# A decoder layer: the cached keys of four sequences turned by VectorE in 32x32 squares and scored on sixteen array tiles

## The chip, the cores and the metric

The kernel runs on one core of one Trainium2 chip. The metric is the device time of one execution in microseconds (us). The engines are named as the profile names them: PE (TensorE, matrix multiplications), PEld (its weight loads), DVE (VectorE), ACT (ScalarE), POOL (GpSimd) and SP (SyncE, which issues nearly all the transfers).

## The reference

The kernel is one step of one decoder layer, for a prompt of 512 rows and for eight sampled sequences of four rows each. The layer is a hybrid mixer (four mLSTM heads beside four heads of differential attention), cross-attention into 256 memory tokens, and a gated MLP with a causal convolution. The change is in the differential attention of the sampled sequences. Each of them has 256 cached rows of keys in two pages, found through a page table, and four new ones:

```python
past_k = cache_dk[l][page_table].reshape(Bs, past_len, DA_HEADS, 2, DA_QK_DIM)   # 8, 256, 4, 2, 64
...
def diff_attend(q, k, v, mask, lam):
    s = jnp.einsum('bqhcd,bkhcd->bhcqk', q.astype(jnp.float32), k.astype(jnp.float32)) * (DA_QK_DIM ** -0.5)
    s = jnp.where(mask[None, None, None], s, -jnp.inf)
    p = jax.nn.softmax(s, axis=-1)
    a = p[:, :, 0] - lam * p[:, :, 1]
    return jnp.einsum('bhqk,bkhd->bqhd', a, v.astype(jnp.float32))
```

A head has 128 numbers in a key: two components of 64. A query gives a score with each component. With four heads, two components and four rows there are 32 rows of scores for each sequence, and 260 columns.

## The kernel before

The kernel is written as Python generators that a framework records in program order; it then sorts the instructions of each engine by priority, adds the semaphores, and each engine runs its own list in that order. Nothing overtakes within an engine, so an instruction that waits holds those behind it.

The stage around the change lies at 247 to 304 us. Two pipelines run in it, one step of each in turn. `pipe(n, *stages)` runs stage s of item t - s in step t, the last stage first.

- The prompt pipeline has 16 items, one for each block of 128 query rows and each head. `da_soft` (L1202) scores both components into two PSUM tiles `sda` (L1211, with the causal mask added by L1212); DVE takes the negated maximum of each (`nm`, L1214), ACT the exponential (`pda`, L1215), and DVE combines both components: the reciprocal (L1217), the coefficient `rc` (L1218) and `pda` (L1219). Two steps later `da_turn` transposes `pda` on PE (`tpa`, L1227), and one more step later `da_av` multiplies by the values (`oda`, L1237). After each fourth item `da_post` normalises (`dasq`, `dass`, `dat`, `dtm`). The key range grows with the block: 128, 256, 384 and 512 columns.
- The pipeline of the cached keys has eight items, one for each sequence. `dk_load` gathers its two pages into a staging tile. `dk_turn` (L1185) transposes them on PE, eight transposes of 128x128 into the PSUM tiles `tpk` (L1191), which ACT and DVE copy to `kT` (L1192). POOL adds the four new keys (L1187). `dk_scores` (L1194) multiplies with `qz`, the queries laid out with zeros so that both components come out of one multiplication: four multiplications, one for each head, on four column tiles of the array (`ssc`, L1197). DVE adds the mask of the four new columns (L1199) and takes the maximum (`snm`, L1035); ACT takes the exponential into `das` (L1036).

When all eight sequences are done, `sample_softmax` makes the coefficients on DVE (`scf`, L1042 to L1045; `csz`, L1046), and PE combines the scores of all sequences (`spa`, L1055). ACT copies the result (`spc`, L1057), DVE makes `pz` from it (L1261), PE transposes both (`spt`, `npn`), ACT lays them out (`daz`), and the loop over the values begins (`ops`, L1279), with the prompt's remaining steps in between. Then comes the output projection, whose weights (`w_out`) are loaded into the same staging tiles.

The slots `kT` come from the pool `wp`, four slots of 8 KB per partition that hold the weights in the other stages (`wslot`). In this stage the weights may use two of them.

## Time and profile before

| | |
|---|---|
| Median of three runs | 957.77 us (955.96 to 959.61) |
| The profiled execution | 956.79 us, its span 955.0 us |
| Busy in the span | PE 932.7, PEld 810.6, DVE 599.2, ACT 388.8, POOL 197.5 us |
| The clock granted to PE | 0.993 over the span, 1.00 in this stage |
| Transfers | 130.27 MB, 136 GB/s on average |

The span is the stretch between the first and the last instruction that the profiler recorded. Busy time is the sum of the stretches in which an engine had an instruction under way. Matrix multiplications are pipelined, so that a busy PE need not be PE at its peak; the distance from the start of one group to the start of the next says what a group holds PE for. Idle time of an engine counts only where another engine waits for it.

### The profile page before, as it was taken

The page shows a single profiled execution, that of the slowest core. Times are in us where ns is not written, and L with a number is a line of the kernel's source. Part 1 is how long each engine was busy: PE and PEld are TensorE (multiplying, and loading weights), DVE is VectorE, ACT ScalarE, POOL GpSimd, SP SyncE. Part 2 cuts the span into 40 slices and gives each one's busy share as a digit, 9 for nine tenths or more (in the row PEclk, how much of TensorE's full clock was granted, in tenths as well). Part 3 has the DMA queues.
Part 4 walks back from the last instruction along what each step waited for, and adds up shares of the span by engine and source line. Part 5 has one row for each costly group of instructions (what it writes and reads, how often), then busy time and mean ns, then how long its engine had stood idle before and what let it go on. Part 6 is the DMA issues. An engine that isn't in the chain of part 4 may idle for free. (4 is left out here: it accounts for less than half of the span.)

```text
span 955.0 us, 17088 instructions
## 1 busy us (share of the span) xinstructions
PE 932.7 (98%) x6619; PEld 810.6 (85%) x6619; DVE 599.2 (63%) x1129; ACT 388.8 (41%) x750; POOL 197.5 (21%) x383
## 2 busy tenths in 40 slices
PE   8999999999999999999999999999999999999995
PEld 5899777879866778998777799989988997999974
DVE  5745144565887448635654769727758676676867
ACT  5655133344676447624544523332212222222232
POOL 6610000024432217300000444001110110111114
PEclk9999999999999999999999999999999999999998
DMA  8950023334825429955953743063053302512023
GB/s 278 309 184 2 1 89 136 89 110 150 264 90 183 155 94 329 307 155 167 353 213 114 206 134 89 4 177 89 4 144 79 122 26 79 165 48 89 24 92 116
DMA packets 120674, 130.27 MB, mean 136 GB/s; under 512 B 8568, under 2 KB 86233, under 8 KB 120593
## 3 DMA queue, kind: packets, MB, share of 16 engines
q1 hardware_dynamic: 114408, 125.69, 41.9%
q10 hardware_dynamic: 6184, 3.48, 1.2%
q8 instruction: 52, 0.85, 0.4%
q14 instruction: 30, 0.24, 0.1%
HBM read 112.22 MB, written 16.93 MB: 135 GB/s over the span
## 5 line engine op out<-in xcount | busy, mean ns | idle before, releaser
L146 ACT CAST wslot<-wst 128x1024 fp32r<-128x1024 f32 x125 | 130.9, 1050 | 259.9 <-issue 74.7
L477 PE MATMUL mm<-fT,wslot 128*128 128x256 f32 x1872 | 235.9, 288 | 0.0
L477 PEld LDWEIGHTS mm<-fT,wslot 128*128 128x128 f32 x1872 | 234.4, 188 | 1.8 <-issue 0.8
L147 DVE TENSOR_TENSOR wslot<-wst,wslot 128x1024 fp32r<-128x1024 f32 x125 | 155.1, 1245 | 89.3 <-ACT wslot L146 88.8
L1691 PE MATMUL mm<-wslot,act 128*128 128x512 f32 (+1 forms) x180 | 70.2, 391 | 0.0
L1692 PE MATMUL mm<-wslot,act 128*128 128x512 f32 (+1 forms) x180 | 70.0, 392 | 0.0
L1690 PE MATMUL mm<-wslot,act 128*128 128x512 f32 (+1 forms) x180 | 69.3, 387 | 0.0
L1598 POOL COPY cvo<-u 128x2 f32<-128x2 f32 x43 | 11.0, 256 | 204.8 <-DVE u L1596 194.7
L407 PE MATMUL mm<-wslot,hT 128*128 128x512 f32 x128 | 52.2, 408 | 0.0
L409 PE MATMUL mm<-wslot,hT 128*128 128x512 f32 x128 | 51.5, 403 | 0.0
L408 PE MATMUL mm<-wslot,hT 128*128 128x512 f32 x128 | 51.3, 401 | 0.0
L477 PE MATMUL mm<-hT,wslot 128*128 128x256 f32 (+1 forms) x384 | 51.0, 289 | 0.0
L1593 DVE TENSOR_TENSOR u<-mm,rsb 128x256 f32<-128x256 f32 x43 | 18.2, 424 | 51.0 <-PE mm L477 50.1
L477 PEld LDWEIGHTS mm<-hT,wslot 128*128 128x128 f32 x384 | 49.2, 188 | 0.5 <-issue 0.2
L1690 PEld LDWEIGHTS mm<-wslot,act 128*128 128x128 f32 x180 | 34.3, 191 | 8.0 <-issue 0.8
L1691 PEld LDWEIGHTS mm<-wslot,act 128*128 128x128 f32 x180 | 33.8, 188 | 7.2
L1692 PEld LDWEIGHTS mm<-wslot,act 128*128 128x128 f32 x180 | 33.8, 188 | 7.2 <-issue 0.4
L1610 ACT ACTIVATE c<-c 128x560 f32<-128x560 f32 x21 | 14.1, 672 | 56.7 <-DVE c L1604 56.7
L1604 DVE SCALAR_TENSOR_TENSOR c<-u,cvT,c 128x560 f32<-128x560 f32 x43 | 34.3, 798 | 0.9
L1603 DVE SCALAR_TENSOR_TENSOR c<-u,cvT,c 128x560 f32<-128x560 f32 x43 | 34.1, 793 | 0.2
L1703 DVE TENSOR_TENSOR yp<-mm,yp 128x512 f32<-128x512 f32 (+1 forms) x41 | 27.2, 674 | 5.1 <-PE mm L1692 5.0
L409 PEld LDWEIGHTS mm<-wslot,hT 128*128 128x128 f32 x128 | 24.5, 191 | 5.3
(474 smaller groups left out, 1857.7 us busy)
## 6 DMA issues: line engine op xcount, KB each, us to landing
wst<-in_w_up_dram SPq DMA_DIRECT2D x42, 512.0 KB
wst<-in_w_in_dram SPq DMA_DIRECT2D x28, 512.0 KB
wst<-in_w_down_dram SPq DMA_DIRECT2D x20, 512.0 KB
wst<-in_cache_mem_k_dram SPq DMA_DIRECT2D x16, 512.0 KB
wst<-in_w_mk_dram SPq DMA_DIRECT2D x8, 512.0 KB
xb<-in_x_prompt_dram SPq DMA_DIRECT2D x8, 512.0 KB
wst<-in_cache_dk_dram SPq DMA_DIRECT2D x16, 256.0 KB
wst<-in_cache_dv_dram SPq DMA_DIRECT2D x16, 256.0 KB
```

Source lines behind the costliest of these rows:

```text
L146: nc.scalar.copy(out=hi, in_=src)
L147: (eng or nc.vector).tensor_tensor(out=lo, in0=src, in1=f32(hi), op=SUB)
L407: mm(ps[b], lhsT=xt.hi(k, c0, c0 + n), rhs=s[:, 0, kk, :], start=(k == 0), stop=False)
L408: mm(ps[b], lhsT=xt.hi(k, c0, c0 + n), rhs=s[:, 1, kk, :], start=False, stop=False)
L409: return mm(ps[b], lhsT=xt.lo(k, c0, c0 + n), rhs=s[:, 0, kk, :], start=False, stop=(k == nk - 1))
L477: mm(ps[i], lhsT=s[:, l, k, :], rhs=x(k, c0, c1), start=(k == 0 and j == 0), stop=(k == 7 and j == 2))
L1603: STT(out=c, in0=u[:, 1:EXT - 1], scalar=w[1], in1=c, op0=MUL, op1=ADD)
L1604: STT(out=c, in0=u[:, 0:EXT - 2], scalar=w[0], in1=c, op0=MUL, op1=ADD)
L1690: mm(ps, lhsT=t[:, 0, c0:c0 + P], rhs=s[:, 0, i % 2, cs], start=st, stop=False)
L1691: mm(ps, lhsT=t[:, 0, c0:c0 + P], rhs=s[:, 1, i % 2, cs], start=False, stop=False)
L1692: return mm(ps, lhsT=t[:, 1, c0:c0 + P], rhs=s[:, 0, i % 2, cs], start=False, stop=en)
L1703: VTT(out=y, in0=ps, in1=y, op=ADD)
```

## The change

For sequences 4 to 7, and for these alone, the keys are no longer turned on PE. `dk_turn` issues one instruction of DVE, which turns the staging tile of 128x1024 in squares of 32x32 into `kq`, one sequence in each prompt step, placed behind the last `nm` of that step. A square's rows are then 32 of the 128 numbers of a head, and the four quarters of the partitions hold different cached rows. So `dk_quads`, in the step in which sequence 7 was scored before, multiplies for all four sequences at once: 64 multiplications of 32x32 weights with 256 columns, on sixteen tiles of the array, four quarters of the numbers added up in PSUM. For each of the four row tiles there is a PSUM tile `ssq` of its own. Four small multiplications score the 16 new keys.

The scores are copied out of PSUM to `das` by ACT and DVE, two tiles each; DVE adds the mask, takes one maximum for the four sequences, and ACT takes four exponentials out of SBUF.

The queries must lie on all four quarters of the partitions for that: `qrep`, a tile of the pool `npool`, is filled through DRAM, one write and four reads, issued by SP. And `kq` takes the place of two of the four weight slots: the pool `wp` is closed at the start of the stage and opened again as `wa` and `wb` of two slots each, `wb` gives way to `kq` for sequences 4 to 7 and comes back behind `dk_quads`. The `kT` of sequences 0 to 3 use the two slots of `wb`.

In `da_soft` the coefficient `rc` is made by a `scalar_tensor_tensor` with one pointer scalar instead of a `tensor_scalar` with two.

```diff
     def dk_turn(b):
-        kt = kts[b] = wp.tile([P, H, 260], F32, name="kT", tag="W")
+        if b >= 4:
+            if b == 4:
+                closed("wb")
+                opened("k", 1)
+                kq.append(lay["k"][1].tile([P, 4, 2, 512], F32, name="kq", tag="K"))
+            with tc.issue_after(dve_last[0]):
+                nc.vector.transpose(kq[0][:, b - 4].rearrange("p g n -> p (g n)"), kst[b][2])
+            return
+        kt = kts[b] = slot([P, H, 260], F32, "kT", "wb")
...
+    qrep = N("qrep", 512).rearrange("p (h j n) -> p h j n", h=H, j=4)
+    qz_d = dram.tile([P, H, NS], F32, name="qz_d")
+    dma(out=qz_d, in_=qz[:, :, 1].rearrange("p h c r -> p h (c r)"))
+    for i in range(4):
+        dma(out=qrep[NS * i:NS * i + NS], in_=qz_d.rearrange("(j q) h n -> q h j n", q=NS))
+
+    def dk_quads():
+        ps = [(at if i else mmp)("ssq") for i in range(4)]
+        kt = kq[0].rearrange("p b g (j r) -> p (b g) j r", r=NS)
+        t = pe_last[0]
+        for j in range(4):
+            for i in range(4):
+                r = slice(NS * i, NS * i + NS)
+                for h in range(H):
+                    with burst(t):
+                        t = mm(ps[i][NS * h:NS * h + NS, :256], lhsT=qrep[r, h, j, :], rhs=kt[r, :, 4 * h + j, :],
+                               start=(j == 0), stop=(j == 3)).ins
+        pn = ps[0][:, 256:272]
+        for h in range(H):
+            with burst(t):
+                t = mm(pn[NS * h:NS * h + NS], lhsT=qz[:, h, 1].rearrange("p c r -> p (c r)"), rhs=dkT[:, h, SEQ + 16:SEQ + 32],
+                       start=True, stop=True).ins
+        VTT(out=sall[:, 4:8, 256:260], in0=v2(pn, TS), in1=con("cm4").unsqueeze(1).broadcast_to([P, 4, TS]), op=ADD)
+        for i in range(4):
+            (VCP if i % 2 else nc.scalar.copy)(out=sall[:, 4:8, :256].rearrange("p b (c i r) -> p b c i r", c=2, i=4)[:, :, :, i, :],
+                                               in_=ps[i][:, :256].rearrange("p (b c r) -> p b c r", c=2, r=NS))
+        VRED(out=nm[:, 4:8], in_=sall[:, 4:8, :], axis=AX.X, op=MAX, negate=True)
+        for b in range(4, 8):
+            ACT(out=sall[:, b, :], in_=sall[:, b, :], func=AF.Exp, bias=nm[:, b:b + 1], accum_out=su[:, b:b + 1])
+        closed("k")
+        opened("wb", NSLOT - 2)
+        slots_in("wb", "wb", "wa", "wa")
+
     def dk_scores(b):
+        if b >= 4:
+            if b == 7:
+                dk_quads()
+            return
...
-        VTS(out=rc[:, 1:2], in0=rc[:, 1:2], scalar1=su[:, 0:1], scalar2=nlam, op0=MUL, op1=MUL)
+        STT(out=rc[:, 1:2], in0=rc[:, 1:2], scalar=nlam, in1=su[:, 0:1], op0=MUL, op1=MUL)
...
     W.nslots = 2
+    closed("w")
+    opened("wa", 2)
+    opened("wb", NSLOT - 2)
+    slots_in("wa")
```

Three places of the engines' lists show what moves (the new kernel's lines are 70 to 75 higher than the old one's).

PE, from the prompt scores of the step in which sequence 7 is scored. First before, then now:

```order
L1211 MATMUL sda<-dkT,dqz 128x384
L1212 LDWEIGHTS cb
L1212 MATMUL sda<-cb 128x128
L1197 MATMUL ssc<-kT,qz 32x260 x4
L1237 MATMUL oda<-dvN,aT 128x128 x2
L1227 MATMUL tpa<-cpk,pda 128x128 x2
L1211 MATMUL sda<-dkT,dqT 128x384
```

```order
L1281 MATMUL sda<-dkT,dqz 128x384
L1282 LDWEIGHTS cb
L1282 MATMUL sda<-cb 128x128
L1240 MATMUL ssq<-kq,qrep 32x256 x64
L1245 MATMUL ssq<-dkT,qz 32x16 x4
L1307 MATMUL oda<-dvN,aT 128x128 x2
L1297 MATMUL tpa<-cpk,pda 128x128 x2
L1281 MATMUL sda<-dkT,dqT 128x384
```

The last sequence's four multiplications have given way to the 68 of the four sequences; the prompt's work around them is as it was, and between it and `spa` stand the same two prompt steps.

DVE, two prompt steps in the middle of the stage. First before (a copy of `kT`, the mask and the maximum of a sequence among the prompt's work), then now:

```order
L1192 COPY kT<-tpk 128x4x128
L1214 TENSOR_REDUCE nm<-sda 128x1
L1199 TENSOR_TENSOR ssc<-ssc,cpk 128x4
L1035 TENSOR_REDUCE snm<-ssc 128x1
L1214 TENSOR_REDUCE nm<-sda 128x1
L1217 RECIPROCAL rc<-su 128x2
L1214 TENSOR_REDUCE nm<-sda 128x1
L1218 TENSOR_SCALAR rc<-rc,su,nlam 128x1
```

```order
L1284 TENSOR_REDUCE nm<-sda 128x1 x2
L1212 STREAM_TRANSPOSE kq<-wst 128x1024
L1287 RECIPROCAL rc<-su 128x2
L1284 TENSOR_REDUCE nm<-sda 128x1
L1288 SCALAR_TENSOR_TENSOR rc<-rc,nlam,su 128x1
L1284 TENSOR_REDUCE nm<-sda 128x1
L1212 STREAM_TRANSPOSE kq<-wst 128x1024
L1289 SCALAR_TENSOR_TENSOR pda<-pda,rc 128x256
```

In each step one long turn stands where a copy, a mask and a maximum stood.

DVE, from the step in which sequence 7 is scored to `csz`. First before, then now:

```order
L1035 TENSOR_REDUCE snm<-ssc 128x1
L1217 RECIPROCAL rc<-su 128x2
L1218 TENSOR_SCALAR rc<-rc,su,nlam 128x1
L1219 SCALAR_TENSOR_TENSOR pda<-pda,rc 128x384
L1042 RECIPROCAL scf<-ssu 128x8
L1214 TENSOR_REDUCE nm<-sda 128x1
L1044 TENSOR_SCALAR scf<-scf,cv 128x8
L1214 TENSOR_REDUCE nm<-sda 128x1
L1045 TENSOR_TENSOR scf<-scf,cpk 128x8
L1046 TENSOR_TENSOR csz<-cpk,scf 128x4x2x16
```

```order
L1289 SCALAR_TENSOR_TENSOR pda<-pda,rc 128x384
L1249 COPY das<-ssq 128x4x2x32 x2
L1247 TENSOR_TENSOR das<-ssq,cpk 128x4x4
L1251 TENSOR_REDUCE snm<-das 128x4
L1284 TENSOR_REDUCE nm<-sda 128x1
L1062 RECIPROCAL scf<-ssu 128x8
L1284 TENSOR_REDUCE nm<-sda 128x1
L1064 TENSOR_SCALAR scf<-scf,cv 128x8
L1065 TENSOR_TENSOR scf<-scf,cpk 128x8
L1066 TENSOR_TENSOR csz<-cpk,scf 128x4x2x16
```

The copies, the mask and the maximum of all four sequences now stand right ahead of the coefficients. On ACT the four exponentials stand together behind the copies, ahead of the prompt's next exponential.

More of the change, by code (lines that the diff above doesn't have):

```diff
@@ L97, with opened, closed, slots_in @@
     sm = ctx.enter_context(tc.tile_pool(name="sm", bufs=4))
+    lay, turns = {}, ["w"]
+    def opened(key, bufs):
+        c = tc.tile_pool(name=f"{key}{len(lay)}", bufs=bufs, side="right")
+        lay[key] = (c, c.__enter__())
+    def closed(key):
+        lay.pop(key)[0].__exit__(None, None, None)
+    def slots_in(*keys):
+        turns[:] = keys
+    def slot(shape, dt, name, key=None):
+        if key is None:
+            key = turns.pop(0)
+            turns.append(key)
+        return lay[key][1].tile(shape, dt, name=name, tag="W")
+    opened("w", NSLOT)
+    ctx.callback(lambda: [closed(key) for key in list(lay)[::-1]])
     psm = ctx.enter_context(tc.tile_pool(name="psm", bufs=5, space=bass.MemoryType.PSUM))
@@ L212, in slot_tile @@
     def slot_tile():
-        return wp.tile([P, 2, 1024], F32R, name="wslot", tag="W")
+        return slot([P, 2, 1024], F32R, "wslot")
     def split_w(sv, st, share):
@@ L1200, in dk_scores @@
         sample_exp(sall, b, ps, nm, su)
+    pe_last, dve_last = [None], [None]
     def da_soft(i):
@@ L1411, in mk_turn @@
         if c == 0:
-            kts[b] = wp.tile([P, 8, 256], F32, name="kT", tag="W")
+            kts[b] = slot([P, 8, 256], F32, "kT")
         for q in range(2):
@@ L1430, in mv_load @@
         if 2 < b < 7:
-            t = wp.tile([P, 2, DM], F32, name="vt", tag="W")
+            t = slot([P, 2, DM], F32, "vt")
             vts[b] = [t[:, 0], t[:, 1]]
```

8 lines of the change are left out of this document (4 added, 4 removed).

## The prediction

> **What bounds the kernel now.** I read the page's busy shares first, then the stretches around the change, then the order of time on PE, DVE and ACT there.
>
> ```profile
> PE 932.7 (98%) x6619; PEld 810.6 (85%) x6619; DVE 599.2 (63%) x1129; ACT 388.8 (41%) x750; POOL 197.5 (21%) x383
> ```
>
> PE is busy 98% of the span, so over the whole kernel any time taken from PE would count. But the change sits in one stage, and there the share is another one. Columns of the next view: stretch, its length, then busy us of PE, PEld, DVE, ACT, POOL, the granted clock, DMA share.
>
> ```profile
> 263.30:276.30 13.00, 12.38 (x102) 8.42 (x99) 11.56 (x34) 10.35 (x36) 3.75 (x5) 1.00 0.42 140
> 276.30:280.90 4.60, 4.60 (x29) 3.04 (x25) 3.80 (x14) 3.77 (x14) 1.95 (x2) 1.00 0.17 59
> 280.90:285.80 4.90, 4.20 (x40) 2.52 (x40) 3.63 (x11) 3.37 (x17) 2.54 (x3) 1.00 0.00 0
> 285.80:304.20 18.40, 18.34 (x206) 11.61 (x206) 13.37 (x23) 13.66 (x32) 2.01 (x3) 1.00 0.69 237
> ```
>
> From the scores of sequence 3 to those of sequence 7 (263.3 to 276.3) DVE works 11.56 of 13.0 us: it is nearly as full as PE. From 285.8, where `ops` begins, PE has no gap left, and the loads of `w_out` wait for the staging tiles that `ops` frees. So I measure the change by one point: when PE reaches `ops`. What that moves, I take the end to move by.
>
> **What PE loses and gains.** PE in order of time: start, length, and the count.
>
> ```profile
> 263.25 1.09 PE L1191 MATMUL tpk<-cpk,wst 128*128 128x128 f32 x8
> 264.18 0.39 PE L1237 MATMUL oda<-dvN,aT 128*128 128x128 f32 x2
> 275.76 0.65 PE L1197 MATMUL ssc<-kT,qz 128*32 128x260 f32 x8
> 276.34 0.71 PE L1237 MATMUL oda<-dvN,aT 128*128 128x128 f32 x4
> 280.94 1.09 PE L1055 MATMUL spa<-das,csz 128*32 128x260 f32 x16
> 285.76 0.85 PE L1279 MATMUL ops<-wst,daz 128*32 128x128 f32 x22
> ```
>
> Eight transposes hold PE 0.93 us (263.25 to 264.18), so 32 of them 3.7. One sequence's scores hold it 0.58 (275.76 to 276.34), four 2.3. Removed: 6.0 us.
>
> Added: 64 multiplications in tiles of 32x32, each of two passes as the eight entries of `ssc` for four multiplications show. A pass of 260 columns takes 0.22: `spa` has two passes more on each of its four tiles than `ssc` and is 1.09 - 0.65 = 0.44 longer. Each of the sixteen tiles has eight passes. If all sixteen run side by side that is 8 x 0.22 plus a load of 0.11, 1.9 us; if only the four of one row of tiles do, 16 groups x 0.44 = 7.0. I take 2.5, near the low end, because of the loads in the next fence: eight of them fit into 0.16 us, 7 ns after one another, and 256 loads and passes at 7 to 10 ns come to 1.8 to 2.6. The four small ones on the new keys add 0.1.
>
> ```profile
> 275.76 0.16 PEld L1197 LDWEIGHTS ssc<-kT,qz 128*32 128x32 f32 x8 [0.37 <-ACT aT L1229]
> 276.54 0.17 DVE L1199 TENSOR_TENSOR ssc<-ssc,cpk 128x4 f32<-128x4 f32 x1
> 277.40 0.48 ACT L1036 ACTIVATE das<-ssc,snm 128x260 f32<-128x260 f32 x1
> 278.31 0.20 DVE L1042 RECIPROCAL scf<-ssu 128x8 f32<-128x8 f32 x1
> 279.64 0.29 DVE L1046 TENSOR_TENSOR csz<-cpk,scf 128x128 f32<-128x128 f32 x1
> 280.94 0.60 PEld L1055 LDWEIGHTS spa<-das,csz 128*32 128x32 f32 x16 [0.37 <-DVE rc L1217]
> 282.31 0.37 ACT L1057 COPY spc<-spa 128x260 f32<-128x260 f32 x1
> ```
>
> A rule speaks against this price. The Trainium skill ("TensorE: Matmul & The Clock Gate", Part 3 on packing small matmuls) says that a weight load overlaps running matmuls only where its row group differs. By it, each tile's eight loads of about 0.11 would lie bare, the block would take 3.4 and the sum below would be 0.9 worse. The trace does not bear it out: the sixteen loads of `spa`, all on the full rows, take 0.60 while its multiplications run, and its 1.09 is four passes, one load and a tail.
>
> **What DVE loses and gains.** Groups by shape, 256 to 284 us: busy us, then mean ns of one.
>
> ```profile
> L1192 DVE COPY kT<-tpk 128x512 f32<-128x512 f32 x5 | 3.4, 686 | 0.0
> L1214 DVE TENSOR_REDUCE nm<-sda 128x1 f32<-128x256 f32 x8 | 3.4, 423 | 0.7 <-PE sda L1212 0.5
> L1214 DVE TENSOR_REDUCE nm<-sda 128x1 f32<-128x384 f32 x6 | 3.3, 548 | 0.7 <-PE sda L1212 0.6
> L1035 DVE TENSOR_REDUCE snm<-ssc 128x1 f32<-128x260 f32 x7 | 3.0, 425 | 0.3 <-DVE ssc L1199 0.2
> L1218 DVE TENSOR_SCALAR rc<-rc,su,nlam 128x1 f32<-128x1 f32 x9 | 2.4, 270 | 0.2
> L1219 DVE SCALAR_TENSOR_TENSOR pda<-pda,rc 128x256 f32<-128x256 f32 x4 | 1.9, 478 | 0.0
> L1219 DVE SCALAR_TENSOR_TENSOR pda<-pda,rc 128x384 f32<-128x384 f32 x3 | 1.8, 616 | 0.1
> L1217 DVE RECIPROCAL rc<-su 128x2 f32<-128x2 f32 x9 | 1.4, 155 | 0.0
> L1076 DVE TENSOR_REDUCE dass<-dasq 128x4 f32<-128x512 f32 x2 | 1.4, 676 | 0.0
> L1083 DVE TENSOR_TENSOR dtm<-dat,gT 128x512 f32<-128x512 f32 x1 | 0.7, 692 | 0.0
> L1036 ACT ACTIVATE das<-ssc,snm 128x260 f32<-128x260 f32 x7 | 3.4, 492 | 1.0 <-DVE rc L1217 0.7 <-DVE snm L1035 0.3
> ```
>
> In a stream each starts 0.08 before the one ahead has ended, as the second and third row of this fence show; its first and last bound the stretch.
>
> ```profile
> 263.38 0.17 DVE L1199 TENSOR_TENSOR ssc<-ssc,cpk 128x4 f32<-128x4 f32 x1
> 269.56 0.47 DVE L1219 SCALAR_TENSOR_TENSOR pda<-pda,rc 128x256 f32<-128x256 f32 x1
> 269.96 0.42 DVE L1035 TENSOR_REDUCE snm<-ssc 128x1 f32<-128x260 f32 x1
> 277.78 0.62 DVE L1219 SCALAR_TENSOR_TENSOR pda<-pda,rc 128x384 f32<-128x384 f32 x1
> ```
>
> No row shows the turn in squares. The nearest, 128x1024 in SBUF, are a scaling and a subtraction, and for the new `rc` form a single column:
>
> ```profile
> L318 DVE TENSOR_SCALAR hN<-xb,rs 128x1024 f32<-128x1024 f32 x4 | 3.0, 750 | 4.8 <-POOL rs L304 4.8
> L147 DVE TENSOR_TENSOR wslot<-wst,wslot 128x1024 fp32r<-128x1024 f32 x97 | 119.0, 1231 | 60.5 <-ACT wslot L146 60.1
> L1246 DVE SCALAR_TENSOR_TENSOR cv<-cpk,nlam 128x1 f32<-128x1 f32 x1 | 0.2, 220 | 5.7 <-POOL nlam L617 5.7
> ```
>
> I take 1.23 less the overlap, 1.15; the low end is 0.75, the high one twice 1.23, were squares filled and emptied in turn. The Trainium skill ("Vector Engine (DVE) Microarchitecture Reference", 3.8) has the square transpose sustain one element per cycle per lane, which would be about 1.1 by its clock; no run here shows that yet.
>
> Between 263.38 and the end of the last row (278.40) DVE passes 15.0 us. Afterwards it issues there, from the order: four turns 4.6, six reductions of 256 columns at 0.34 and two of 384 at 0.47, 3.0; one `snm` 0.34; four `pda` of 256 at 0.40 and one of 384 at 0.54, 2.1; `dass` and `dtm` 1.2; five reciprocals at 0.08 and five `rc` at 0.14 (the new form saves 0.05 each), 1.1. That is 12.4 us, against PE's 12.4 - 4.6 = 7.8 (20 of the transposes and the four scores lie in this stretch): here DVE now decides. With half a microsecond of waits it takes 12.9. It also starts 0.9 earlier, because eight of the transposes stand right ahead of sequence 3's scores. PE's last `sda` before the block is needed by a reduction that ends 1.3 us before the stretch does, so the sixteen-tile block begins at about 274.3 instead of 275.76: **1.5 us earlier**, of the 5.4 that PE is spared by then (3.7 and three scores).
>
> **The tail.** Before, last scores to `spa`: 275.76 to 280.94, 5.2 us, and `csz` was ready 1.0 before (279.93). Afterwards all four sequences finish at once: block 2.6 and 0.2 to the first copy; two copies of 128x256 out of PSUM on DVE while ACT does two, 0.75 by the 0.42 row; the mask 0.1; one maximum over 4 x 260 columns, by 0.125 us for each 128 columns (0.548 - 0.423) 0.425 + 0.76 = 1.2; four exponentials one behind the other on ACT, 4 x 0.48 less some overlap, 1.85; then `scf` to `csz`, 278.31 to 279.93 less one of the two prompt reductions between them, 1.1. Sum 7.8: `spa` at 282.1, 1.2 later. PE has only 4.6 us of prompt work to put beside these (the stretch 276.3 to 280.9), and its last `sda` there waits for an exponential that now stands behind the four on ACT. DVE too is held by `scf`, with prompt reductions behind it, so that `spc`, and `pz` behind `dass` and a `pda`, come some 0.5 later still. Together **+1.7 us** at `ops`.
>
> **What costs nothing.** The write of `qz_d`, four reads into `qrep`, and the pool's closing and opening:
>
> ```profile
> L1167 POOL COPY qz<-dqT x2: 291/783/1275, 197.9 to 199.2; 64x128 f32<-64x128 f32 x2
> 197.19 2.24 SPq L254 DMA_DIRECT2D wst<-in_w_in_dram  x2
> 207.44 0.92 SPq L916 DMA_DIRECT2D wst<-in_state_ml_C_dram  x2
> 232.09 1.93 PE L962 MATMUL mlsi<-wst,qzm 128*32 128x128 f32 x64
> ```
>
> SP would stand at `qz_d` until `qz` is there, at 199.5, with one load of `w_in` behind it; SP's next issue is at 207.44. The four `qrep` reads push the state loads by some 2 us (0.5 each); PE wants these at 232. The keys 0 to 3 have two slots instead of whichever is free, each used after the scores two sequences back. The cover gone, each would cost its 1 to 2 us.
>
> **Rivals.** *Faster, as PE decides:* if a turn costs 0.75 and the block 1.9, DVE's stretch shrinks by 1.6, the block starts at 272.7, `spa` at 279.9, a gain of 1.0; with nothing but PE in the way, 5.4 earlier and 2.0 longer (2.6 for 0.58), 3.4. DVE's 12.4 of work speaks against. It decides below 1.0 us a turn. *Row tiles do not overlap:* the block takes 7.0, 4.4 more. The loads at 7 ns speak against; nothing here uses two row tiles at once. *Turns at half rate:* 4 x 1.3 = 5.2 more on DVE. *The chain from the block is hidden and nothing changes* lies inside my forecast's spread.
>
> **How the numbers follow.** The profiled execution took 956.79 (span 955.0 and 1.8 around it), 1.0 under the median of the runs, 957.77. The sum gives 958.5 by the one and 959.5 by the other; I say 959.0, base 957.3. Chances: the tail decides, +0.3 to +3.5 (957.6 to 960.8), 0.57; faster, 953.9 to 956.8, 0.26; row tiles one after another, 963.4, 0.08; turns at half rate, 964.2, 0.09. The range 954.5 to 962.0 leaves out the last two and the edge of the second. About 0.5%, 4.8 us, is what a measurement can tell from no change: below 953.0 falls hardly anything, 0.02; above 962.6 most of the last two, 0.12.
>
> **What would show it.** DVE with almost no idle between 262 and 275, turns near 1.2 us; the block of `ssq` near 2.5 us and starting near 274; ACT's four exponentials in a row, DVE idle over a microsecond before `scf`, PE idle ahead of `spa` near 282, `ops` near 287.5. It is wrong if the turn or the block has another price, or if PE finds waits at the block (its four PSUM tiles, three of which `dat` and `spa` share).

## The result, and the profile after

The change makes the kernel slower: 969.96 us (968.07 to 971.41, four runs) against 957.25 before (four runs), a ratio of 1.0123 [1.0096, 1.0151]. The prediction was 959.0, with a range up to 962.0. On two other chips the same kernel took 964.18 (1.0084 [1.0058, 1.0111]) and 968.38 us (1.0113 [1.0093, 1.0132]). The profiled execution took 971.41 us, its span is 969.6.

The first view is the page of the kernel after: what the engines do in the span, and the clock granted to PE in 40 slices.

```profile
PE 939.5 (97%) x6691; PEld 814.0 (84%) x6691; DVE 603.5 (62%) x1125; ACT 387.5 (40%) x748; POOL 194.8 (20%) x379
PEclk9999999999999999999989989999999999999998
```

PE was busy 6.8 us longer than before, although it has some 3 us less to do (6.0 removed, 2.9 added). The second row says where to look: before, every slice but the last shows a 9. Now two more show an 8, the slices from 485 and from 558 us. A slice is 24 us long, so a stretch of a few us hides in it. Columns of the next view: stretch, length, busy us of PE, PEld, DVE, ACT and POOL, the granted clock, DMA share, GB/s. The first three rows are the kernel before, the rest after.

```profile
260.00:264.00 4.00, 3.42 (x30) 2.60 (x31) 3.88 (x12) 3.59 (x13) 2.18 (x4) 1.00 0.76 251
500.00:504.00 4.00, 4.00 (x19) 3.27 (x18) 1.06 (x2) 0.22 (x1) 0.00 (x0) 1.00 0.01 4
558.00:561.00 3.00, 3.00 (x27) 3.00 (x26) 1.83 (x6) 1.80 (x4) 3.00 (x5) 1.00 0.79 285
260.00:264.00 4.00, 3.19 (x17) 1.69 (x16) 3.80 (x11) 2.11 (x8) 0.50 (x2) 0.63 0.22 77
264.00:268.00 4.00, 1.98 (x11) 1.46 (x10) 3.64 (x11) 2.63 (x9) 0.00 (x0) 0.93 0.45 140
268.00:272.00 4.00, 4.00 (x18) 3.16 (x16) 2.73 (x7) 1.60 (x6) 2.42 (x3) 0.59 0.35 124
496.00:500.00 4.00, 3.65 (x13) 2.46 (x12) 4.00 (x12) 1.94 (x6) 0.00 (x0) 0.57 0.00 0
500.00:504.00 4.00, 4.00 (x11) 3.09 (x11) 1.70 (x8) 0.27 (x1) 0.00 (x0) 0.58 0.00 0
558.00:561.00 3.00, 2.12 (x10) 2.12 (x11) 3.00 (x3) 1.53 (x3) 1.04 (x3) 0.50 0.52 183
561.00:565.00 4.00, 4.00 (x21) 4.00 (x21) 4.00 (x6) 0.77 (x3) 2.53 (x4) 0.52 0.81 219
```

PE ran at half its clock for stretches of some us. The missing share times the length of the rows gives 3.4 us in the key stage (4 x 0.37 + 4 x 0.07 + 4 x 0.41), 3.4 at 496 to 504 and 3.4 at 558 to 565. The prediction had no term for it. What stands ahead of these places shows in PE's rows; in brackets is the idle time and what ended it.

```profile
259.11 0.30 PE L1297 MATMUL tpa<-cpk,pda 128*128 128x128 f32 x1 [1.34 <-DVE pda L1289]
261.25 1.10 PE L1265 MATMUL ssc<-kT,qz 128*32 128x260 f32 x8 [0.81 <-DVE rc L1287]
267.26 0.44 PE L1297 MATMUL tpa<-cpk,pda 128*128 128x128 f32 x2 [2.02 <-DVE pda L1289]
274.27 0.41 PE L1297 MATMUL tpa<-cpk,pda 128*128 128x128 f32 x2 [1.19 <-DVE pda L1289]
495.56 0.44 PE L1573 MATMUL ost<-cpk,oS 128*128 128x128 f32 x2 [2.11 <-ACT oS L1570]
558.88 5.49 PE L485 MATMUL mm<-fT,wslot 128*128 128x256 f32 x24 [1.27 <-POOL fT L167]
```

PE waits for DVE in the key stage, and twice more, some 200 and 300 us behind the change. The eight scores at 261.25, which take 0.65 at full clock, take 1.10; the 24 products at 558.88 are those that took 3.1 in the second profile, where the clock held.

To see where time goes in each kernel, I take the start of eight rows that all have, and the end. Before and after (the stage's first prompt scores, the last scores or the block, `spa`, `ops`, the first product of the queries of the cross-attention, `ost`, `rsb`, the first `cvo`); the three of before that the prediction shows, and the `ost` of after, which stands above, are not repeated:

```profile
247.68 0.38 PE L1211 MATMUL sda<-dkT,dqT 128*128 128x128 f32 x2
383.42 1.31 PE L465 MATMUL mm<-hqT,wslot 128*128 128x256 f32 x9
489.09 0.44 PE L1499 MATMUL ost<-cpk,oS 128*128 128x128 f32 x2
545.26 0.82 PE L1566 MATMUL rsb<-cpk,rsd 32*128 32x32 f32 x4
598.72 0.27 PE L1659 MATMUL cvo<-cpk,cvo 128*72 128x128 f32 x1
245.93 0.38 PE L1281 MATMUL sda<-dkT,dqT 128*128 128x128 f32 x2
276.07 2.76 PE L1240 MATMUL ssq<-kq,qrep 32*32 32x256 f32 x128
284.88 1.09 PE L1075 MATMUL spa<-das,csz 128*32 128x260 f32 x16
290.36 0.65 PE L1353 MATMUL ops<-wst,daz 128*32 128x128 f32 x16
389.19 1.07 PE L485 MATMUL mm<-hqT,wslot 128*128 128x256 f32 x7
554.79 0.40 PE L1640 MATMUL rsb<-cpk,rsd 32*128 32x32 f32 x2
611.65 0.27 PE L1733 MATMUL cvo<-cpk,cvo 128*72 128x128 f32 x1
```

The table gives how much longer each stretch between two such starts is than in the kernel before (us of one profile each, worked out from those rows; the last column is the difference of the spans). The lower rows belong to the experiments.

```
                    stage   to     to    to    to     to    to     to     to     span
                    starts  block  spa   ops   hqT    ost   rsb    cvo    end
after, 1st profile  -1.75  +2.06  +3.63 +0.66 +1.17  +0.70 +3.06  +3.40  +1.67  +14.6
after, 2nd          -0.85  -0.33  +3.62 +0.66 +1.05  +0.17 +1.61  +0.91  +0.86   +7.7
after, 3rd          -0.62  -0.31  +3.62 +0.66 +1.57  +0.85 +0.98  +2.08  +0.87   +9.7
rc alone            -1.30  +1.33  -0.24 -0.06 +0.08  +0.43 -0.38  -0.13  -0.03   -0.3
pools alone         -0.91  +0.11  +0.01 -0.01 +2.50  +2.21 +0.29  +0.92  +0.18   +5.3
rc and pools        -2.12  +1.41  +0.01 -0.06 +2.72  +0.81 +0.69  -0.11  +0.35   +3.7
turn behind pda     +0.12  +1.31  +4.80 +3.05 +2.22  +0.13 +0.35  +1.69  +0.73  +14.4
PE filler           +0.50  +1.30  +4.15 +1.42 +2.18  +0.89 +1.00  +1.36   0.00  +12.8
after, old rc       -1.17  -0.96  +4.26 +1.25 +1.73  +1.15 +2.15  +1.17  +1.52  +11.1
split maxima        -0.50  -0.33  +3.08 +2.85 +1.78  +0.28 +0.33  +1.82  +0.69  +10.0
half turn           -1.03  -1.94  +3.62 +0.66 +0.58  +0.73 +1.14  +2.23  +0.71   +6.7
gaps filled         -1.63  +0.21  +7.86 +0.71 +1.35  +1.26 +0.76  -0.15  +0.13  +10.5
 and split maxima   +0.60  +0.23  +7.05 +0.80 +1.26  +1.20 +0.27  -0.03  -0.18  +11.2
late gaps filled    -1.79  +2.18  +3.63 +0.66 +5.59  +1.18 -0.74  +0.56  -0.07  +11.2
 and split maxima   -1.53  -0.33  +3.08 +2.73 +1.37  +1.05 +0.50  +0.76  +0.27   +7.9
```

The first column is mostly a matter of single executions: the profile of before itself has one stretch of half clock, at 96 us, worth 1.7. The third column is the same in every execution of the changed kernel: +3.62 from the block to `spa`. The rest varies from one execution of one kernel to the next, by 7 us in the span, and the stretches that vary most are those with half clock.

### The profile page after: what moved, and what is told of

Same layout as the page of the kernel before. It is cut to its first block, busy times and chain, and to the rows that moved or that the text cites. A ratio compares the mean times of both kernels' runs of the same rounds, so it can differ in the third digit from the quotient of the medians.

```text
span 969.6 us, 17225 instructions
## 1 busy us (share of the span) xinstructions
PE 939.5 (97%) x6691; PEld 814.0 (84%) x6691; DVE 603.5 (62%) x1125; ACT 387.5 (40%) x748; POOL 194.8 (20%) x379
## 5 line engine op out<-in xcount | busy, mean ns | idle before, releaser
L167 DVE TENSOR_TENSOR wslot<-wst,wslot 128x1024 fp32r<-128x1024 f32 x125 | 155.5, 1249 | 95.3 <-ACT wslot L166 95.0
L485 PE MATMUL mm<-fT,wslot 128*128 128x256 f32 (+1 forms) x192 | 28.2, 309 | 1.5 <-POOL fT L167 1.3
```

The costliest lines, as they stand in the source:

```text
L167: (eng or nc.vector).tensor_tensor(out=lo, in0=src, in1=f32(hi), op=SUB)
L485: mm(ps, lhsT=s[:, l, k, :], rhs=x(k, c0, c1), start=(k == 0 and j == 0), stop=(k == 7 and j == 2))
```

## The experiments

The theories went from letter to letter as the runs came in. A, B and C were the first: the stage's waits cost the clock (A), the stage is late by its waits alone and the clock falls by chance (B), the late losses come from the new places in memory (C). D and E ask what the fused `rc` and the new pools cost by themselves, F whether the tail sets the end, H whether DVE's row sets the start of the block. Theory G (half clock follows places where PE idles) is what was left for the clock at the end.

**The changed kernel again.** No edit.

> The changed kernel once more, unaltered, for a second profile of it. Theory A (the waits of PE for the prompt's pda in the key stage let the throttle grant half the clock, and this belongs to the change): half clock again between 258 and 274 us after a PE wait on pda, ops some 4 to 6 us later than in the kernel before, time 968 to 972. Theory B (the stage is late by its waits alone; the half clock falls by chance): the same time within 2 us, but stretches of half clock elsewhere or fewer than the 10.2 us of PE time that they took in the first profile. Theory C (the later losses at 495 and 558 us come from the new slots and order of memory): both later PE waits (2.1 at ost, 1.3 at fT) return with or without half clock.

964.18 us, six below the first measurement. A single stretch of half clock came, at 495 us; none in the key stage, although PE waited there just as long (1.34, 0.81, 2.33, 1.42 us). So A's "half clock again between 258 and 274" failed. C's two later waits did return. B came nearest, though its time missed as well: the second profile tells that a longer path is there without half clock, and that half clock comes and goes.

**Pools and rc without the turns.** All keys on PE as before; `qrep` with its write and four reads is left out too (the edit shows the main places):

```diff
     def dk_turn(b):
-        if b >= 4:
...
-            return
         kt = kts[b] = slot([P, H, 260], F32, "kT", "wb")
...
     def dk_scores(b):
-        if b >= 4:
-            if b == 7:
-                dk_quads()
-            return
...
+    slots_in("wb", "wb", "wa", "wa")
     aw, az = sample_softmax(sall, su, cv, con("selD"), "da")
```

> The new slot pools, the order of slots after the stage and the fused rc alone; all eight sequences' keys are turned and scored on PE as in the kernel before, no copy of qz. Theory A: 957 plus or minus 1.5, clock at 1.00 from 256 to 570. Theory B: the same. Theory C: 962 to 967, with PE's waits and half clock at 495 and 558 as in the changed kernel, and the key stage unchanged (ops near 286).

960.92 us, 1.0053 [1.0031, 1.0075]. All three theories missed: there is no half clock between 15 and 940 us, and yet half of the changed kernel's loss on this chip (3.7 of 7.0 by the medians) is there, with no key turned on DVE. By the table it is late at the last scores (+1.41), between `ops` and the cross-attention (+2.72) and ahead of `ost` (+0.81).

**The turn behind the STT of pda.**

```diff
-            dve_last[0] = VRED(out=nm[:, c:c + 1], in_=sv[c], axis=AX.X, op=MAX, negate=True).ins
+            VRED(out=nm[:, c:c + 1], in_=sv[c], axis=AX.X, op=MAX, negate=True)
...
-        STT(out=pt[:, 0, :nk], in0=pt[:, 1, :nk], scalar=rc[:, 1:2], in1=pt[:, 0, :nk], op0=MUL, op1=ADD)
+        dve_last[0] = STT(out=pt[:, 0, :nk], in0=pt[:, 1, :nk], scalar=rc[:, 1:2], in1=pt[:, 0, :nk], op0=MUL, op1=ADD).ins
```

> The changed kernel with each turn issued behind the STT that finishes pda of the step, in place of behind the two maxima, so that the tpa transposes don't wait through a turn. Theory A: PE's waits on pda fall from 4.5 us in three to under 2, no half clock before 280, ops 2 to 4 us earlier against the stage's start, time 959 to 965. Theory B (DVE is full either way, a turn moved is only a wait moved): ops within 1 us of the changed kernel's, time 967 to 972.

970.83 us, 1.0156 [1.0127, 1.0185]. Worse, so A's cure was wrong: some of the `pda` came earlier, but the last turn slid to 275.81, behind the `pda` of its step, and the block had to wait for it.

```profile
275.81 1.23 DVE L1212 STREAM_TRANSPOSE kq<-wst 128x1024 f32<-128x1024 f32 x1
277.19 4.05 PE L1240 MATMUL ssq<-kq,qrep 32*32 32x256 f32 x128 [3.29 <-DVE rc L1287]
```

Behind 3.29 us of idle the block ran mostly at half clock: 4.05 against 2.76 us.

**Filler for PE in the stage.**

```diff
         tp = mmp("tpa")
+        for _ in range(3 if i in (3, 5, 7) else 0):
+            mm(tp[:, :512], lhsT=dkT[:, h, 0:P], rhs=dkT[:, h, 0:512], start=True, stop=True)
```

> The changed kernel with nine matmuls of 512 columns that nobody reads (0.6 us each, 5.2 us of PE in all) ahead of the tpa transposes of heads-steps 3, 5 and 7, where PE waited 1.3, 2.0 and 1.2 us. Theory A: the granted clock stays at 1.00 from 256 to 290, and ops comes at most 5 us later than in the kernel before though PE does 5.2 us more; time 964 to 970. Theory B: the filler beyond the 4.5 us of waits adds to the chain, ops as late as in the changed kernel or up to 2 us later, time 970 to 974, clock no matter.

967.99 us, 1.0116 [1.0088, 1.0144]. The clock stayed at 1.00 from 256 to 290 and the time fell into A's range, but half clock came at 499 and 560, and the unfilled second profile kept its clock in the stage too. This run decides little.

**The parts: rc, pools, and the change without rc.** The first is the kernel before with this edit; the second the kernel of "pools and rc without the turns" with the edit undone; the third the changed kernel with it undone.

```diff
-        VTS(out=rc[:, 1:2], in0=rc[:, 1:2], scalar1=su[:, 0:1], scalar2=nlam, op0=MUL, op1=MUL)
+        STT(out=rc[:, 1:2], in0=rc[:, 1:2], scalar=nlam, in1=su[:, 0:1], op0=MUL, op1=MUL)
```

> The kernel before with the fused rc alone (STT in place of VTS; nothing else of the change). Theory D (the order of instructions that the scheduler settles on is worth microseconds, and the fused rc alone moves it: maxima, kT copies, pda and tpk change places from 257 us on, and the last 32 of ops are cut in two by an sda): 958.5 to 961, the loss standing by 303 us. Theory E (rc is worth what it saves, 0.05 us in a step, and the 3.7 us of the kernel with the pools and rc alone come from the pools): 957.2 plus or minus 1.

958.69 us, 1.0024 [1.0011, 1.0036]: slower by 2.3 by the ratio, as D said. (Its one profile, 956.46, is its fastest run and doesn't show the loss as a whole, only that the last scores come 1.33 later against the stage's start.) The scheduler puts maxima, copies and transposes in another order, as D had it, but the traces show something else first. The old form of `rc` reads one tensor, the fused one two (`rc` and `su`). Here is the `rc` of the same step in the kernel before and in this one, each while a product of two tensors runs on POOL (257.64 to 258.92, 256.74 to 258.03):

```profile
258.49 0.27 DVE L1218 TENSOR_SCALAR rc<-rc,su,nlam 128x1 f32<-128x1 f32 x1
257.07 0.97 DVE L1218 SCALAR_TENSOR_TENSOR rc<-rc,nlam,su 128x1 f32<-128x1 f32 x1
```

The copy behind it (`xts`) grows from 0.22 to 1.28, and the maximum of sequence 2 begins 1.6 later against the stage's start (14.29 for 12.68). In the changed kernel it begins 1.47 later, and with the old `rc` put back not later at all (both from their profiles). So the fused form costs DVE time at the place where it meets POOL; how much of the 2.3 is that and how much the order was not measured.

> The kernel before with the new slot pools alone (rc as before, all keys turned on PE). Theory D: 957.5 to 959.5, since the order of the key stage changes little, and what is lost stands between 481 and 492 us, where pso waits for a value load and cvT copies go in between pT's on VectorE. Theory E: 960 to 962, most of the loss by 303 us through the two slots that kT is left with.

960.84 us, 1.0037 [1.0025, 1.0049]: the time is in E's range, the place is neither's alone, for the table has +2.50 between `ops` and the cross-attention and +2.21 ahead of `ost`. In its profile PE waits where the kernel before waits less or not at all: 2.3 us at `pso` (0.9 before) and 1.6 at the prompt's last scores (none). Two stretches of half clock follow, at 484 and 553 us.

```profile
PE pso L1475 <- DMA wst<-in_cache_mem_v_dram: 2.3, 1, 2.3
PE sda L1235 <- ACT pda L1239: 1.6, 1, 1.6
```

So both parts that the prediction took as free cost microseconds: 1 to 3.4 and 2.4 to 4.7 by the intervals, and 3.0 to 7.2 in the kernel that has both. What in the pools costs it, the two slots or the order in which the weights take them, was not tested.

> The changed kernel with rc computed as before (VTS); turns, block and pools kept. Theory D: 961 to 963, 1 to 3 us less than the changed kernel on the same chip (964.2), for rc's share of the loss goes. Theory E: 964 plus or minus 1, or up to 0.5 more.

969.66 us, 1.0140 [1.0119, 1.0162]: D's 961 to 963 missed; they were set against the changed kernel on another chip, and on this one it was not measured. The block did come earlier (-0.96 against the stage's start, where the fused rc gives -0.3), though this profile has half clock at 265.7 us, ahead of it. But the tail took 0.6 more, `ops` 0.6, and the stretches behind it gave the rest back. Effects of order don't add up from one kernel to another.

**One maximum per sequence in the tail.**

```diff
-        VRED(out=nm[:, 4:8], in_=sall[:, 4:8, :], axis=AX.X, op=MAX, negate=True)
         for b in range(4, 8):
+            VRED(out=nm[:, b:b + 1], in_=sall[:, b, :], axis=AX.X, op=MAX, negate=True)
```

> The changed kernel with one maximum per sequence (four of 260 elements, some 0.4 us each) in place of one of 1040 (1.24), so that the first exp starts behind the first maximum. Theory F (the tail from the block to spa, 8.8 us against 5.2 for the last score before, is on the path that sets the end): spa and ops 0.7 to 1.0 us earlier against the start of the block, total 0.5 to 1.2 less than the changed kernel's. Rival (DVE's own row in the prompt's steps sets the end, the tail has slack): ops unchanged within 0.2, total the same.

969.01 us, 1.0134 [1.0112, 1.0156]. `spa` came 0.54 earlier (+3.08 for +3.62; 0.7 was the least expected), but from there to `ops` it took 2.2 more (+2.85 for +0.66): behind the tail's waits half clock fell from 287 to 290.4.

```profile
283.50:287.00 3.50, 1.98 (x23) 0.97 (x16) 3.19 (x10) 3.09 (x16) 1.81 (x3) 1.00 0.00 0
287.00:290.40 3.40, 3.40 (x13) 2.30 (x12) 1.63 (x3) 0.71 (x4) 0.44 (x1) 0.51 0.00 0
290.40:300.00 9.60, 9.60 (x116) 6.01 (x115) 4.68 (x10) 4.52 (x12) 1.38 (x1) 0.99 0.65 194
```

These three rows show the whole pattern: PE idles 1.5 us of 3.5, then runs 3.4 us at half clock, then at full clock again. That made theory G.

**The base, the gaps filled, half a turn.** One chip. The fillers stand in the waits: four or three of them ahead of `tpa` of steps 3, 5 and 7, ahead of the second `sda` of step 10, ahead of `ost`, and behind the first product with `fT`. The second edit is from the half turn: it turns only the first half of a sequence's keys and leaves out the second, and the block reads the first half twice (that line isn't shown).

```diff
+    def fill(ps, n, w=300):
+        for _ in range(n):
+            t = mm(ps[:, :w], lhsT=ident, rhs=cpk[:, 0:w], start=True, stop=True)
+        return t.ins
...
-                nc.vector.transpose(kq[0][:, b - 4].rearrange("p g n -> p (g n)"), kst[b][2])
+                nc.vector.transpose(kq[0][:, b - 4, 0], kst[b][0])
```

> The changed kernel unaltered, as the base of this group on one chip. Theory G (two parts: a longer path of some 7 to 8 us that every execution has, and stretches of half clock of 1.71 us each, which follow about every second place where PE idles 1.25 us or more within 3.5; the changed kernel has five or six such places before 940 us, the kernel before one): time less the clock's loss within 2 us of the other profiles of this kernel, 5 or 6 such places, 1 to 4 of them followed by half clock; 964 to 970 us.

968.38 us. Six places, two of them followed by half clock, as G said. The third profile's late rows:

```profile
491.40:494.90 3.50, 1.18 (x11) 0.85 (x9) 3.17 (x3) 3.50 (x6) 0.00 (x0) 0.98 0.64 241
494.90:498.20 3.30, 3.30 (x12) 2.77 (x13) 3.30 (x8) 1.87 (x6) 0.00 (x0) 0.50 0.01 4
552.40:556.10 3.70, 1.40 (x8) 0.99 (x8) 3.70 (x4) 2.42 (x4) 3.48 (x3) 1.00 0.49 142
556.10:559.50 3.40, 3.40 (x17) 3.40 (x18) 3.40 (x6) 2.30 (x5) 1.65 (x5) 0.52 0.60 185
```

> The changed kernel with 22 unread matmuls of 300 columns (0.3 us each, about 7 us of PE) put into PE's six waits: three ahead of tpa, one ahead of the sda in the tail, one ahead of ost, one ahead of the first product with the lower half of fT. Theory G: at most two places with 1.25 us of idle in 3.5 are left, at most one stretch of half clock between 15 and 940 us, mean clock back at 0.993 to 0.995, and 2 to 5 us less than the changed kernel beside it, in spite of 7 us more work of PE. Rival (the clock falls by chance or by heat, whatever PE's waits are): as many stretches of half clock as beside it, and the time the same or up to 5 us longer.

968.12 us, the same as the base. The clock did as G said: 0.994 as a mean of the runs (base 0.988, kernel before 0.994), no half clock between 15 and 940 us, and the stretch from `rsb` to `cvo` that had cost 2.08 was back at -0.15. But G's time, 2 to 5 less, missed: four places were left (at most two were expected), and the tail with the filler in it grew (`spa` +7.86 instead of +3.62). The clock's 5 us came back and the tail took 4.2.

> The changed kernel with each turn of 512 elements in place of 1024 (the block scores the first half twice; the second half of the keys is left out), so VectorE has 4 times 0.6 = 2.4 us less and all else is alike. Theory H (in the key stage VectorE is full and its row sets when the block begins): block 1.8 to 2.6 us earlier against the stage's start, ops likewise, time 2 to 3 us less. Rival (PE's own order and waits set it): block and ops less than 0.8 us earlier, time within 1 us.

965.92 us, 1.0089 [1.0073, 1.0104], 2.5 under the base. A turn took 0.70 instead of 1.23, 2.1 for four, and the block began 1.6 earlier (-1.94 for -0.31): most of what DVE was spared reached the block. H holds, though its least for the block was 1.8: DVE's row decides there.

> The filled kernel with one maximum per sequence in the tail. Theory G: spa 0.5 us earlier than in the filled kernel, and now the end too, 0.3 to 1 us, since no half clock takes the gain. Rival (tail has slack): the same time as the filled kernel within 0.3.

966.81 us, 1.0096 [1.0078, 1.0113], 1.3 less than with the gaps filled. `spa` came 0.8 earlier. That the end kept it isn't shown: the two intervals overlap, and the spans of the two profiles differ the other way.

**The late gaps alone.** The same fillers, only ahead of `ost` and at `fT`.

> The changed kernel with eight unread matmuls of 300 columns in PE's two late waits alone (ahead of ost near 492 us, and ahead of the first product with the lower half of fT near 553 us); the key stage is left as it is. Theory G (half clock follows PE's idle places): no half clock between 480 and 570 us, mean clock 0.990 to 0.993 against 0.988, and the stretch from 545 to 600 us within 0.5 us of the kernel before's; time 1.5 to 3.5 us less than the changed kernel (968.4 on the last chip). Rival (the clock falls whatever PE waits for): half clock there as before, time the same.

965.12 us, 1.0077 [1.0064, 1.0091]. The changed kernel had 1.0113 [1.0093, 1.0132] on the chip of the base and 1.0084 [1.0058, 1.0111] on that of the second profile, so whether time was gained isn't shown. The clock did what G said: no half clock between 480 and 570 us, PE idle 0.4 of the first 30 us and 0.2 of the second:

```profile
480.00:510.00 30.00, 29.62 (x246) 21.94 (x246) 18.58 (x45) 14.40 (x37) 0.00 (x0) 1.00 0.63 233
540.00:570.00 30.00, 29.78 (x187) 25.61 (x186) 23.99 (x43) 15.49 (x30) 14.94 (x27) 1.00 0.72 213
```

> The same with one maximum per sequence in the tail (spa 0.5 us earlier). Theory G: 0.3 to 1.5 us less than with the late gaps filled alone, unless half clock falls near 287 us, behind the tail's waits, as in the earlier run with split maxima. What is left above the kernel before is then path: 5 to 8 us.

967.73 us, 1.0097 [1.0079, 1.0115]: no gain over the late gaps alone. In its profile half clock fell at 286.5 us, the exception that was named.

**Holes in the kernel before.** If idle places cause half clock, the kernel before must show it too. The longer holes have 5 and 7 in place of the 3:

```diff
+    def hole():
+        hs = Z("hs")[:, :300]
+        ps = at("hole")
+        with burst(mm_last[0]):
+            mm(ps[:, :300], lhsT=ident, rhs=cpk[:, 0:300], start=True, stop=True)
+            nc.scalar.copy(out=hs, in_=ps[:, :300])
+            for _ in range(3):
+                nc.scalar.copy(out=hs, in_=hs)
+            return mm(ps[:, :300], lhsT=ident, rhs=hs, start=True, stop=True).ins
```

> The kernel before with PE made to wait at four places of the feed-forward part, where it has no wait: a matmul of 300 columns, four ACT copies in a chain, and a matmul that reads the last copy (1.5 to 2 us of idle each; a fifth place is filled by other work). Theory G: one to three of the four are followed by half clock for 3.4 us; mean clock falls from 0.994 to 0.988 to 0.992; time 8 to 12 us more than before (four times 1.75 us of wait and 0.3 of work, and 1.71 for each stretch of half clock). Rival (no link between waits and clock): no half clock there, 6 to 8.5 us more.

969.79 us. The holes were only 1.3 us long and no half clock followed; mean clock 0.994. G's forecast missed, and so did the rival's time: 12.3 more in place of 6 to 8.5, since the waits were only 4.5 of it and the ten added matmuls with their chains cost more than I had counted.

> As with the holes before, but with six ACT copies in each chain: PE idles 2.2 us in place of 1.3 at the four places. The holes of 1.3 us were followed by no half clock and took 12.3 us in all. Theory G, as it now stands (1.6 us of idle or more in 3.5 is followed by half clock about every second time, 1.3 seldom): one to three of the four are followed by half clock, mean clock 0.988 to 0.992, and 5 to 9 us more than with the shorter holes (4 times 0.92 of wait, 1.71 for each stretch). Rival (no link): 3.5 to 4.5 us more and no half clock between 600 and 900 us.

977.15 us, 7.4 over the short holes (on another chip, where the kernel before took 957.23 for 957.49), mean clock 0.9906: one of four was followed by half clock in the profile.

> Eight copies in each chain: PE idles 3.1 us at the four places. Theory G: three or four of the four followed by half clock, mean clock 0.985 to 0.989, and 12 to 15 us more than with the holes of 1.3. Rival: 7 to 8.5 us more and no half clock there.

982.60 us, 12.8 over the short holes, mean clock 0.9886: all four were followed. Two of the holes, with the 3 us behind each:

```profile
633.50:637.00 3.50, 0.29 (x4) 0.16 (x1) 0.00 (x0) 2.97 (x8) 0.00 (x0) 0.94 1.14 306
637.00:640.00 3.00, 3.00 (x11) 2.68 (x12) 0.00 (x0) 0.00 (x0) 0.00 (x0) 0.50 1.09 357
711.50:715.50 4.00, 1.18 (x16) 0.52 (x16) 0.95 (x2) 3.50 (x8) 0.00 (x0) 0.95 1.12 303
715.50:718.50 3.00, 3.00 (x11) 2.67 (x12) 0.00 (x0) 0.00 (x0) 0.00 (x0) 0.50 1.13 282
```

Both times lie in G's ranges and outside the rival's. None of the other seventeen profiles has half clock between 600 and 900 us, so here the waits caused it: shown for waits of 3 us, which lie above those of the changed kernel, and for one of four of 2 us.

## Why the prediction was wrong

Three steps failed: the sum up to `ops`, the rule that the end moves by as much as `ops`, and the clock, which had no term.

**Prices of the new instructions: right, one of them by luck.** A turn takes 1.23 us and 1.16 from start to start (I took 1.15). By the Trainium skill ("Vector Engine (DVE) Microarchitecture Reference", 3.8) I had estimated 1.1; the trace agrees within a tenth. The block takes 2.69 us (276.07 to the new keys at 278.76 in the first profile) where I took 2.5, so row tiles do run side by side, and two rivals fall: no 7.0 us block and no turn at half rate. 128 passes of 0.22 would be 28.2 us one after another; 28.2 / 2.69 is 10.5, and the Trainium skill ("TensorE: Matmul & The Clock Gate", Part 3) has 10.6 measured for sixteen tiles. The weight loads are not all hidden, though: in the first profile's records they come in four bursts, which begin at 0, 0.65, 1.30 and 1.94 us of the block, where the two passes of a burst would take 0.43. By the Trainium skill's rule on weight loads (same part) I would have had 3.4, which is too much. But the 7 to 10 ns for each load, from which I took 2.5, do not set the pace. What holds the loads back stays open.

**DVE decides: right in kind, short in size.** I had the block begin 1.5 us earlier. It begins 0.3 earlier in the executions with full clock. From the mask of sequence 3 to the end of the `pda` of 384 columns beside the block DVE passed 14.0 us in the second profile (263.03 to 277.06) instead of my 12.9: the eight maxima held it 3.4 instead of 3.0, reciprocals and `rc` 1.5 instead of 1.1, and it waited 0.74 instead of 0.5. And it started 0.5 later against the stage's start, not 0.9 earlier. Most of the late start goes with the fused `rc`: with it alone the scores of sequence 3 come 0.96 later (262.33 - 246.38 against 262.67 - 247.68), and in the changed kernel with the old `rc` the block begins 0.96 earlier, nearer to what I had forecast. I had priced `rc` by the 0.05 us that it saves, and not by the 0.97 that it takes beside a product on POOL and the order that it upsets.

**The tail: 8.8 instead of 7.8.** DVE, ACT and PE of the third profile, from the first copy to `spa`:

```profile
277.49 0.76 DVE L1249 COPY das<-ssq 128x256 f32<-128x256 f32 x2 [0.18 <-PE ssq L1240]
278.36 0.37 ACT L1249 COPY das<-ssq 128x256 f32<-128x256 f32 x1 [0.41 <-DVE das L1247]
278.76 1.24 DVE L1251 TENSOR_REDUCE snm<-das 128x4 f32<-128x1040 f32 x1 [0.44 <-ACT das L1249]
280.04 0.51 ACT L1253 ACTIVATE das<-das,snm 128x260 f32<-128x260 f32 x1 [0.77 <-DVE snm L1251]
282.15 0.20 DVE L1062 RECIPROCAL scf<-ssu 128x8 f32<-128x8 f32 x1 [1.69 <-ACT das L1253]
282.73 0.91 PE L1281 MATMUL sda<-dkT,dqz 128*128 128x384 f32 x2 [1.12 <-ACT pda L1285]
283.15 0.29 DVE L1066 TENSOR_TENSOR csz<-cpk,scf 128x128 f32<-128x128 f32 x1
283.63 1.09 PE L1075 MATMUL spa<-das,csz 128*32 128x260 f32 x16
```

The terms were the right ones: the maximum 1.24 (1.2), the waits on the exponentials where I said, PE's too, which comes to `spa` straight from an `sda` that waited 1.12 us for the exponential behind the four. Missing were 0.4 us in which ACT's second copy waits for the mask on DVE, 0.3 on the four exponentials (2.1 from 280.04 to 282.15, taken as 1.85), 0.2 each from `scf` to the end of `csz` and from there to `spa`. From `spa` to `ops` it is 0.66 longer, where I said 0.5. So `ops` comes 4.0 later against the stage's start (-0.33 + 3.62 + 0.66) instead of the 1.7 that I summed up: the sum failed by 2.3 us, 1.2 of it at the block, 1.0 in the tail, with no half clock in the stage.

**"What that moves, I take the end to move by": wrong.** Behind `ops` another 4.6 and 6.4 us are lost (second and third profile, from `ops` to the end), of which one and two stretches of half clock make 1.7 and 3.4. One part isn't the turns': the stretches to `hqT` and `ost` are longer by 1.2 and 2.4 together, and pools and rc without any turn show a loss of that kind (+2.72 and +0.81). "What costs nothing" is the step that failed there, for the pool's closing and opening; the slots alone cost 1.0037 [1.0025, 1.0049]. What is left, 1.7 and some 0.5 us, lies behind `ost` and stays open. The copies into `qrep` did cost nothing that shows: PE waits nowhere from 190 to 247 us in the profile before and in the first two after, and from `mlsi` to the stage's start it takes 15.59 us in all nineteen.

**The clock: no term at all.** The granted clock was 1.00 in the stage before, and I took it as given. The mean over the timed runs gives an estimate of its share, as if PE were busy throughout: 1 - 0.988 of the span is 11.2 us for the base, 6.3 for the kernel before on that chip: 5 of the 11.3 us. On the chip of the second profile the clock was 0.994 and 0.993, and the loss 7.0 us. So each execution pays some 6 to 8 us by path and order, and up to 5 more on average by clock.

In nineteen profiles I counted the places between 15 and 940 us where PE idles at least 1.25 us in 3.5, in steps of half a microsecond: before one at most, in the changed kernel five or six. Behind places of 1.25 to 1.6 us half clock followed 4 times in 27, of 1.6 to 2.5 us 19 in 47, above 2.5 us 6 in 6. Each stretch lasts 3.41 us and takes 1.71 of PE's time; two may follow one another.

Which of the waits are followed can be read from the clock records: in each of the nineteen traces all changes of the clock lie on one grid of 3.4133 us, within 3 ns. In the first profile the four stretches of half clock behind 15 us begin at 261.05, 267.88, 496.57 and 558.01 us, which are 2, 67 and 18 steps apart. Counted by the windows of that grid, from 100 to 940 us and leaving out those at half clock, PE was idle 1.82 us or more in 21 windows, and half clock followed all 21. Of 24 windows with 1.42 to 1.82 us 7 were followed, of 47 with 1.0 to 1.42 one, of 3825 with less none. So a wait counts by what falls into one window, and the grid lies differently in each execution: of the four holes of some 2 us the one that lay with 2.02 us in one window was followed, the three that were split (1.64, 1.63 and 1.14) were not. The bounds were drawn after the counts were seen, and no run moved a wait against the grid on purpose.

The Trainium skill ("TensorE: Matmul & The Clock Gate", Part 1) has a free-running window of 3413 ns after which the clock goes to 4/8 or back, and no ratio between. The traces agree: the grid of 3.4133 us, and 0.50. The Trainium skill's rule of thumb (same page, "Why this matters for your kernels"), no idle gap above some 3 us, is too lenient here: 1.82 us within one window was enough each time, and the measurement decides.

## What to carry to other kernels

Where PE is at 98%, price the waits that a change makes, not only the work that it moves: a wait of 2 us may cost another 1.7 behind it, at a place where nothing was changed. The parts of the edit that were taken as free cost 2 to 4 us each here, as much as the work that the edit was about; make the "free" parts alone before the rest, and price a new form of an instruction by what it takes beside its neighbours, not only by itself. And one profile of a kernel whose clock varies shows one draw: compare two before explaining a stretch.

## What was not expected of the hardware

Half clock behind idle places far under 3 us, in units of 1.71 us, is told above. Seven of the nineteen profiles have one more such stretch at 95 to 97 us, the one of the kernel before among them, with no idle of PE in the 7 us ahead. Right ahead PE runs a row of eight small products (`dps`, 4 rows deep and 4 or 8 columns wide, 93.93 to 95.87 in the kernel before). In the seven profiles this row, 1.94 us long, lies whole in one window of the grid; in the other twelve a boundary cuts it, and no half clock follows. So PE can be busy all the time and be granted half the clock; that such small products count as idle is the likely reason, but no run varied them. Also open is why the clock's share differs from chip to chip for the same kernel (0.988, 0.994 and 0.988 as means of the runs). And the fused `rc` grew beside a POOL instruction with two inputs: in the first profile, one column took 0.97 us while POOL's products of `L167` were under way (256.30 to 260.50), and 0.20 after them. Over the nineteen profiles it took 0.17 to 0.23 us in 169 places without a product of two tensors on POOL as it began, and in 39 with one 0.85 in the median and up to 1.07. The old form took 0.25 to 0.28 in all 19 places beside one.

```profile
256.64 0.97 DVE L1288 SCALAR_TENSOR_TENSOR rc<-rc,nlam,su 128x1 f32<-128x1 f32 x1
261.42 0.20 DVE L1288 SCALAR_TENSOR_TENSOR rc<-rc,nlam,su 128x1 f32<-128x1 f32 x1
```
